# Decoder layer in full-precision parts: the last pair's steps in the down run, and pair 6's sums, moved to other rows

## The chip, the cores and the metric

One core of one Trainium2 chip runs the kernel. The metric is device time in microseconds of one execution, the median over several executions. A core has TensorE (PE: matmuls into the accumulators in PSUM; PEld is its weight load), VectorE (DVE), ScalarE (ACT), GpSimd (POOL), the queues of SyncE (SP) that issue DMAs, and 16 DMA engines. Each engine works through its own list of instructions in order; semaphores hold an instruction back until what it reads is there.

## The reference, cut to what matters

A decoder layer over 256 tokens of width 2048: a normalised input projection, attention over 8 heads beside a pooling mixer, an output projection, and a gated feed-forward part with a causal convolution of width 3 over the tokens. The change lies in that last part:

```python
def conv_ffn(h, w_up, conv_w, conv_b, w_down):
    u = h @ w_up                                   # (256, 2 * 5632)
    u_pad = jnp.pad(u, ((0, 0), (CONV_WIDTH - 1, 0), (0, 0)))
    y = conv_b
    for i in range(CONV_WIDTH):
        y = y + conv_w[i] * u_pad[:, i:i + S]
    gate, val = jnp.split(y, 2, axis=-1)
    return (jax.nn.silu(gate) * val) @ w_down      # (256, 2048)
```

## The kernel before

**Precision.** All matmuls run on numbers split in two: a high part (a copy rounded by ScalarE) and a low part (the number less its high part, by VectorE). A product is high x high, high x low and low x high. This holds for weights (`wh` at L184, `wl` at L190) and for activations (`hid[..., 0, :]` at L849, `hid[..., 1, :]` at L874).

**Thirds.** The 44 feature blocks of the feed-forward part are done in three thirds of 8, 8 and 6 pairs (a pair is 256 hidden features). A third has an **up run**, in which each pair has a block for its gate and a block for its value (four steps each, TensorE lines L271 and L273), and then a **down run** for the two halves `nb` of the output columns (TensorE line L904). The first step of a down run is called the border here.

**Seven products.** Where a pair is one of `sevens`, its two by two block of products is done with seven instead of eight, on sums of activation blocks and of weight blocks. The sums of the weights are made during the up run and go through memory (`mixed`); the sums of the activations are made by `left_sums`: four subtractions and additions on `y` (L889), a high part on ScalarE (L890) and a low part on VectorE (L891). In the first two thirds pairs 1 to 7 are such, in the order 1, 2, ..., 7, and pair 0 comes last with eight products; in the last third pairs 0 to 4 are such in one half and 0 to 3 in the other, and its last pair, 5, is not. A seven-product pair takes two steps in the down run, one with a weight tile of 2048 columns (`sum`: four products, 12 matmuls) and one of 1536 columns (`rest`: three products, 9 matmuls). An eight-product pair has one tile of 2048 columns.

**Weights.** One weight tile is a row of the plan. At the step at which row c starts on TensorE, the loop at the end of `layer` puts the high part of row c + 3 on ScalarE's list and then the low part of row c + 2 on VectorE's. When the low part is done, the buffer of the raw tile (five in all in this phase) is free, and SyncE issues the next load into it. There are 4 buffers for high and 3 for low parts. All weights come this way, so the order of the loads follows VectorE's order.

**The order is written by hand.** `later(n, f)` puts f at the step n after the one in hand; what is due at a step is put on the engines' lists behind the weights' parts of that step. (In an up run a row takes two steps, and only its first step counts: `later(2, ...)` is one row on. In a down run each seven-product row is one step.) `deferred` holds what is put on at the beginning of the next step, behind what is due there. `pending` holds ScalarE work that waits for the next time that an accumulator is emptied (`add_halves`, L540 and L543), and `firsts` what goes ahead of the weights' parts at a given step.

**A value block** (`value`) ends with `conv_in` (L540, L543, L801): the accumulator is emptied into `u`. Then come `conv` (six instructions on ScalarE, L812 and L814), `taps` (two additions on VectorE, L822), the product with the gate (L848), hid's high part (L849) and low part (L874), and, for a seven-product pair, `left_sums`. For the last pair of a third (`end`) all of it after `conv_in` falls into the down run. In `value`, `at_once` chooses between two orders; it is given by `g >= g1 - 2` inside a lambda. The steps after the border at which the last pair's parts are put on, as the code runs:

| part | thirds 1 and 2 | third 3 |
|---|---|---|
| conv | 0 | 2 and 4 (halves) |
| taps | 4 | 6 |
| gate product, hid's high part | 6 | 7 |
| hid's low part | 8 | 8 |
| four sums, their high part | 9 | - |
| low part of the sums | 11 | - |

The next to last seven-product pair of a third ahead of it (pair 6; pair 4 in the last third) has its four sums four steps before the border; their high part waits in `pending` for the next emptied accumulator, at the step before the border, and their low part comes at the border ahead of the weights (thirds 1 and 2, by `firsts`) or one step behind it (third 3).

Of the kernel before, what the change touches and what calls it, by code (L numbers as in the profile page):

```python
# [25 lines left out]
AF = mybir.ActivationFunctionType  # L26
# [3 lines left out]
P = 128  # L30
D = 2048
S = 256
# [5 lines left out]
NF = DFF // P  # L38
# [62 lines left out]
def layer(ctx: ExitStack, tc: tile.TileContext, xT, wts, mix, par, rel_d, ident_d, icnt_d, out):  # L101
    nc = tc.nc
# [15 lines left out]
    def small(name):  # L118
        return sm.tile([P, 512], F32, name=name, tag="small")
# [3 lines left out]
    def col(c):  # L123
        return pv[:, c:c + 1]
# [10 lines left out]
    late, free, place = {}, [f"raw{i}" for i in range(RAWS)], {}  # L135
# [185 lines left out]
    ps = small("ps_start")  # L321
# [277 lines left out]
    hold, splits, now, agenda, firsts, pending = set(), [], [0], {}, {}, []  # L599
    where = []  # L600

    def later(n, f):
        agenda.setdefault(now[0] + n, []).append(f)
# [25 lines left out]
    def after(u, f):  # L629

        hooks.append((u, f))
# [81 lines left out]
    def scratch(name):  # L713
        return late["pool"].tile([P, 2, S], F32, name=name, tag="fs", bufs=2)
# [82 lines left out]
    def conv_in(ps):  # L797

        s = scratch("fs")
        add_halves(s, ps)  # L800
        nc.vector.tensor_tensor(late["u"][:, :, 2:], s, late["rrow"][:, None, :].to_broadcast([P, 2, S]), op=OP.mult)  # L801

    def conv(f0_, which, apart=None):

        u = late["u"]
        y = late["pool"].tile([P, 2, S], F32, name="y", tag=f"y{which}")
        z = [scratch("z") for _ in range(2)]

        def half_of(m):
            f = f0_ + m  # L810
            cw = [col(C_CW + i * 2 * NF + f) for i in range(3)]
            nc.scalar.activation(y[:, m, :], u[:, m, 2:], AF.Identity, scale=cw[2], bias=col(C_CB + f))  # L812
            for i in range(2):
                nc.scalar.activation(z[i][:, m, :], u[:, m, 1 - i:1 - i + S], AF.Copy, scale=cw[1 - i])  # L814
        half_of(0)
        later(apart, lambda: half_of(1)) if apart else half_of(1)
        return y, z

    def taps(y, z):
# [18 lines left out]
            later(2, lambda: rest(parts))  # L838
        deferred.append(start)

    def value(ps, g, j, seven, end, at_once):
        conv_in(ps)

        def join(y):
            if j == 0:
                late["hid"] = keep.tile([P, KT, 2, S], F32R, name="hid", tag="c")
            hid, ks = late["hid"], slice(2 * j, 2 * j + 2)
            nc.vector.tensor_tensor(y, y, late["gate"], op=OP.mult)  # L848
            pending.append(lambda: nc.scalar.activation(hid[:, ks, 0, :], y, AF.Copy))  # L849
            if end:  # L850
                pending.pop()()
            later(1 if end and at_once else 2, lambda: rest2(y, hid, ks))

        def rest(parts):
            y = taps(*parts)
            if end:
                later(1 if at_once else 2, lambda: join(y))
            else:
                join(y)

        def start():
            if end and at_once:
                later(2, apart)
                return
            parts = conv(NF + 2 * g, 1)
            later(4 if end else 2, lambda: rest(parts))

        def apart():
            parts = conv(NF + 2 * g, 1, 2)
            later(4, lambda: rest(parts))  # L870
        deferred.append(start)

        def rest2(y, hid, ks):
            nc.vector.tensor_tensor(hid[:, ks, 1, :], y, hid[:, ks, 0, :].bitcast(F32), op=OP.subtract)  # L874
            if seven:
                f = lambda: late.__setitem__(("S", j), left_sums(y, end, at_once))
                later(1, f) if end else f()

    def left_sums(y, alone, at_once):

        s = y.rearrange("p a (b n) -> p (a b) n", n=P)
        if alone:
            pair = [late["pool"].tile([P, n], F32R, name="sums7", tag=tag)[:, :512] for n, tag in ((516, "u"), (512, "y0"))]
        else:
            parts = block("sums", F32R)
            pair = [parts[:, :512], parts[:, 512:]]
        pair = [t.rearrange("p (b n) -> p b n", n=P) for t in pair]
        for out_, a, b, op in ((3, 3, 1, OP.subtract), (1, 0, 1, OP.subtract), (0, 3, 0, OP.add), (2, 2, 0, OP.subtract)):
            nc.vector.tensor_tensor(s[:, out_, :], s[:, a, :], s[:, b, :], op=op)  # L889
        pending.append(lambda: nc.scalar.activation(pair[0], s, AF.Copy))  # L890
        low_part = lambda: nc.vector.tensor_tensor(pair[1], s, pair[0].bitcast(F32), op=OP.subtract)  # L891
        if alone:
            pending.pop()()
            later(2, low_part)
        elif at_once:
            later(5, low_part)
        else:
            firsts.setdefault(now[0] + 4, []).append(low_part)
        return pair

    def product(ps, left, right, first, last):
        (ah, al), (wh, wl) = left, right
# [85 lines left out]
    for n, ((g0, g1), sevens) in enumerate(zip(THIRDS, SEVEN)):  # L988
        ups = []
        for g in range(g0, g1):  # L990
            ups.append(feat_block(lambda: late["h"], XK, lambda ps, g=g: gate(ps, g)))
            ups.append(feat_block(lambda: late["h"], XK,
                                  lambda ps, g=g, j=g - g0, sevens=sevens, end=g == g1 - 1: value(ps, g, j, any(j in s for s in sevens), end, g >= g1 - 2)))
        u0 = len(steps)
        steps += [h for b in ups for h in b]
        if n == 0:
            for q in range(4):
                after(u0 + 2 + 3 * q, lambda q=q: x2_turn(q))
        for nb in range(2):
            run = {"n": nb * 1024, "end": n == 2 and nb == 1}  # L1000

            def done(t, lo, m, run=run, n=n, nb=nb):
                x2 = late["x2"][:, t, run["n"] + lo:run["n"] + lo + m]
                c = run["c"][t]
                if m == 1024:
                    parts = [(c[b], x2[:, b * 512:(b + 1) * 512]) for b in range(2)]
                else:
                    parts = [(c[lo // 512], x2)]
                for b, (ps, x) in enumerate(parts):
                    add = lambda ps=ps, x=x: nc.vector.tensor_tensor(x, ps, x, op=OP.add)  # L1010
                    later(3, add) if not nb and t and b else add()
                if n == 2:
                    k = min(m, 768 - lo) if nb and t else m
                    store = lambda: nc.sync.dma_start(out[:, t, run["n"] + lo:run["n"] + lo + k], x2[:, :k])
                    store() if nb else later(9, store)

            run["done"] = done
            run["x2"] = lambda t, b, run=run: late["x2"][:, t, run["n"] + b * 512:run["n"] + (b + 1) * 512]
            fresh0 = {(t, b) for t in range(NT) for b in range(2)}
            js = down_order(g1 - g0, sevens[nb])  # L1020
            for j in js:
                def chunk(u, j=j, nb=nb, run=run, sevens=sevens[nb], js=js, fresh0=fresh0, end=n == 2 and nb == 1):
                    if j == js[0]:
                        run["left"] = set(fresh0)
                        pair = [acc("ps_down") for _ in range(2)]
                        ones_ = [[f("ps_down") for f in (aux, small)] for _ in range(2)]
                        twos = [[t[:, b, :] for b in range(2)] for t in pair]
                        if nb:
                            (p6, p7), (p5, p1), (c10, c00), (c01, c11) = twos + ones_
                            run["c"] = [[c00, c01], [c10, c11]]  # L1030
                        else:
                            run["c"], ((p6, p7), (p5, p1)) = ones_, twos
                        run["p"] = p1, p5, p6, p7
                        run["spare"] = twos[0][0]
                    if j in sevens:
                        seven_mixed(u, j, run, j == sevens[0])
                    else:
                        eight_products(u, j, run, run["left"], j == js[-1], end and j == js[-1])
                        run["left"] = set()
                if j == js[-1]:  # L1040
                    hold.add(len(steps))
                steps.append([chunk])
                steps.append([lambda u, j=j, run=run, sevens=sevens[nb]: j in sevens and
                              seven_rest(u, j, run, j == sevens[0], j == sevens[-1])])
# [3 lines left out]
    n = len(steps)  # L1048
# [113 lines left out]
```

## Time and profile before

| | |
|---|---|
| median of 3 runs | 991.66 us (991.54 to 993.82) |
| the profiled execution | 990.43 us |
| its span, first to last instruction | 988.6 us |
| TensorE busy | 978.5 us, 99% |
| VectorE busy | 882.1 us, 89% |
| ScalarE busy | 630.1 us, 64% |
| granted TensorE clock | 1.00 |
| borders (first L904 matmul of a third) | 458.50, 713.77, 925.51 us |

Times in rows of the profile are microseconds from the start of the span. A row of the timeline has start, duration, engine, line, operation, the tiles written and read, shapes and count, and, where the engine sat idle before it, how long and what ended that. Instructions of one line in a row are merged into one row with their count. A matmul's duration there is longer than the distance to the next, since matmuls are pipelined: distances between starts are what counts. A row of the windows view has, for a stretch, its length, busy time and count of PE, PEld, DVE, ACT and POOL, the granted clock, the DMA engines' share and GB/s. A row of the waits view has who waited for whom, total, times and longest. A row of DMA issues has count, size and median time from issue to landing.

### The profile page before, as it was taken

The numbers are of one execution on the slowest core, as the hardware profiler recorded it, in microseconds if no ns is written. First come the engines' busy times: TensorE is split into PE (matmuls) and PEld (weight loads), VectorE is DVE, ScalarE is ACT, GpSimd is POOL, SyncE is SP. The second block draws the span as 40 slices with busy tenths as digits, with TensorE's granted clock in tenths as the row PEclk, the third lists the DMA queues.
The fourth block names the chain that finished last, engine by engine and source line by source line (L and its number), as shares of the span: only waits on it lengthen the run. The fifth ranks groups of instructions, "written<-read, shape, count | busy, mean of one in ns | idle before, by whom it ended". The sixth has DMA issues, their size and how long they took to land.

```text
span 988.6 us, 13621 instructions
## 1 busy us (share of the span) xinstructions
PE 978.5 (99%) x5249; PEld 844.6 (85%) x5249; DVE 882.1 (89%) x958; ACT 630.1 (64%) x736; POOL 61.3 (6%) x120
## 2 busy tenths in 40 slices
PE   9999999999999999999999999999999999999998
PEld 7888888898888888888788888888887888888887
DVE  6777859988888999998998999999899999999898
ACT  6555445544557766777666666776776746677762
POOL 0202322200002310000000000000000000000000
PEclk9999999999999999999999999999999999999999
DMA  9859878689878899976999999898689989998694
GB/s 355 311 205 344 293 243 287 207 326 390 303 266 304 312 392 394 370 296 251 363 335 362 349 389 367 336 355 333 260 314 323 398 332 347 369 388 329 219 350 163
DMA packets 52577, 317.08 MB, mean 321 GB/s; under 512 B 7112, under 2 KB 9800, under 8 KB 20256
## 3 DMA queue, kind: packets, MB, share of 16 engines
q1 hardware_dynamic: 47824, 304.28, 81.3%
q0 software_dynamic: 4688, 11.94, 4.2%
q8 instruction: 41, 0.67, 0.3%
q14 instruction: 24, 0.20, 0.1%
HBM read 269.13 MB, written 47.06 MB: 320 GB/s over the span
## 4 chain that ended last, share of the span: by engine, by line
PE 96%; DVE 2%; issue 1%; DMA 0%; ACT 0%; SPq 0%; DVEq 0%
PE ps_feat L271 41%; PE ps_feat L273 21%; PE ps_down L904 20%; PE ps_tok L259 9%; PE ps_val L249 4%; DVE wl L190 1%; PE ps_pool L280 1%; PE ps_s L492 1%; DMA raw<-in_wts 0%; ACT wh L184 0%; PE ps_av L528 0%; DVE y L889 0%; PE ps_av L530 0%; PE ps_val L240 0%; DVE x L1010 0%
## 5 line engine op out<-in xcount | busy, mean ns | idle before, releaser
L271 PE MATMUL ps_feat<-x2h,wh 128*128 128x512 f32 x1406 | 478.2, 389 | 0.0
L190 DVE TENSOR_TENSOR wl<-raw,wh 128x2048 fp32r<-128x2048 f32 (+1 forms) x182 | 394.0, 2176 | 12.9 <-ACT wh L184 7.5
L184 ACT ACTIVATE wh<-raw 128x2048 fp32r<-128x2048 f32 (+1 forms) x182 | 331.2, 1829 | 102.5 <-DMA raw<-in_wts 50.4
L273 PE MATMUL ps_feat<-x2h,wl 128*128 128x256 f32 x1408 | 388.6, 276 | 0.0
L271 PEld LDWEIGHTS ps_feat<-x2h,wh 128*128 128x128 f32 x1406 | 263.9, 188 | 54.4
L273 PEld LDWEIGHTS ps_feat<-x2h,wl 128*128 128x128 f32 x1408 | 264.3, 188 | 0.0
L904 PE MATMUL ps_down<-wh,hid 128*128 128x512 f32 (+1 forms) x338 | 116.1, 387 | 0.0
L162 DVE TENSOR_TENSOR wl<-raw,wh 128x2048 fp32r<-128x2048 f32 (+3 forms) x44 | 82.9, 1894 | 35.2 <-ACT wh L161 26.4
L904 PE MATMUL ps_down<-wh,sums 128*128 128x512 f32 x296 | 104.5, 390 | 3.5 <-DVE sums L891 3.5
L540 ACT ACTIVATE fs<-ps_feat 128x512 f32<-128x512 f32 x52 | 31.0, 597 | 105.6 <-DVE y L822 52.3
L271 PE MATMUL ps_feat<-cat,wh 128*128 128x512 f32 x256 | 87.3, 389 | 0.0
L814 ACT ACTIVATE z<-u,pv 128x256 f32<-128x256 f32 x176 | 79.3, 498 | 3.5 <-DVE x L947 3.5
L259 PE MATMUL ps_tok<-wh,xh 128*128 128x512 f32 x256 | 80.1, 391 | 0.0
L161 ACT ACTIVATE wh<-raw 128x2048 fp32r<-128x2048 f32 (+3 forms) x44 | 69.4, 1597 | 13.9 <-DMA raw<-in_wts 10.1
L904 PEld LDWEIGHTS ps_down<-wh,hid 128*128 128x128 f32 x338 | 63.3, 188 | 13.2
L273 PE MATMUL ps_feat<-cat,wl 128*128 128x256 f32 x256 | 70.7, 276 | 0.0
L904 PEld LDWEIGHTS ps_down<-wh,sums 128*128 128x128 f32 x296 | 55.4, 188 | 15.5 <-DVE sums L891 4.2
L904 PE MATMUL ps_down<-wl,hid 128*128 128x512 f32 (+1 forms) x169 | 65.4, 387 | 0.0
L822 DVE TENSOR_TENSOR y<-y,z 128x512 f32<-128x512 f32 x88 | 60.6, 688 | 4.4
L904 PE MATMUL ps_down<-wl,sums 128*128 128x512 f32 x148 | 58.7, 397 | 1.2 <-DVE wl L190 1.2
L259 PEld LDWEIGHTS ps_tok<-wh,xh 128*128 128x128 f32 x256 | 48.1, 188 | 10.0
L271 PEld LDWEIGHTS ps_feat<-cat,wh 128*128 128x128 f32 x256 | 48.1, 188 | 10.0
(184 smaller groups left out, 1061.8 us busy)
## 6 DMA issues: line engine op xcount, KB each, us to landing
raw<-in_wts SPq DMA_DIRECT2D x141, 1024.0 KB, 7.7
raw<-in_mix SPq DMA_DIRECT2D x37, 1024.0 KB, 7.4
mixed<-raw SPq DMA_DIRECT2D x37, 1024.0 KB, 7.4
raw<-mixed SPq DMA_DIRECT2D x37, 1024.0 KB, 6.9
raw<-in_wts SPq DMA_DIRECT2D x37, 768.0 KB, 6.3
raw<-in_wts SPq DMA_DIRECT2D x4, 512.0 KB, 6.5
x2d<-x2x POOLq DMA_DIRECT2D x4, 512.0 KB, 8.0
x<-x2d POOLq DMA_DIRECT2D x32, 64.0 KB, 6.8
```

Source lines behind the costliest of these rows:

```text
L161: nc.scalar.activation(wh, w, AF.Copy)
L162: nc.vector.tensor_tensor(wl, w, wh.bitcast(F32), op=OP.subtract)
L184: nc.scalar.activation(w, raws[c][:, :width(c)], AF.Copy)
L190: nc.vector.tensor_tensor(wl, raws[c][:, :width(c)], wh.bitcast(F32), op=OP.subtract)
L249: nc.tensor.matmul(ps[b][:, t, :], xh[:, k, a, ts], w[:, ws], start=False, stop=(k == KT - 1 and n == 2), skip_group_check=True)
L259: nc.tensor.matmul(ps[:, t, :], act[:, k0 + k, a, ts], w[:, ws], start=(first and k == 0 and n == 0), stop=(last and k == 1 and n == 2))
L271: nc.tensor.matmul(ps, wh[:, ws], act[:, k, :, :], start=(bool(first) and n == 0), stop=False, skip_group_check=True)
L273: nc.tensor.matmul(ps[:, S:], wl[:, ws], act[:, k, 0, :], start=False, stop=(last and n == len(ks) - 1), skip_group_check=True)
L540: nc.scalar.activation(dst, ps[:, :, S:], AF.Copy)
L814: nc.scalar.activation(z[i][:, m, :], u[:, m, 1 - i:1 - i + S], AF.Copy, scale=cw[1 - i])
L822: nc.vector.tensor_tensor(y, y, t, op=OP.add)
L904: nc.tensor.matmul(ps, a, w, start=(first and n == 0), stop=(last and n == 2), skip_group_check=True)
```

## The change

The last pair of each third gets one order, and its ScalarE parts are put on one step behind the VectorE work that they read:

| part | before, thirds 1 and 2 | before, third 3 | after, all thirds |
|---|---|---|---|
| conv | 0 | 2 and 4 | 0 |
| taps | 4 | 6 | 3 |
| gate product | 6 | 7 | 4 |
| hid's high part (ScalarE) | 6 | 7 | 5 |
| hid's low part | 8 | 8 | 6 |
| four sums | 9 | - | 7 |
| their high part (ScalarE) | 9 | - | 8 |
| their low part | 11 | - | 9 |

The pair before the last (`left == 1`, now bound when the lambda is made: pair 6, in the last third pair 4) has both parts of its sums put on two steps before the border. Pairs before it stay as they were.

```diff
-    def conv(f0_, which, apart=None):
+    def conv(f0_, which):
...
-    def value(ps, g, j, seven, end, at_once):
+    def value(ps, g, j, seven, end, late_sums):
...
-            pending.append(lambda: nc.scalar.activation(hid[:, ks, 0, :], y, AF.Copy))
-            if end:
-                pending.pop()()
-            later(1 if end and at_once else 2, lambda: rest2(y, hid, ks))
+            high_part = lambda: nc.scalar.activation(hid[:, ks, 0, :], y, AF.Copy)
+            later(1, high_part) if end else pending.append(high_part)
+            later(2, lambda: rest2(y, hid, ks))
 
         def rest(parts):
             y = taps(*parts)
-            if end:
-                later(1 if at_once else 2, lambda: join(y))
-            else:
-                join(y)
+            later(1, lambda: join(y)) if end else join(y)
 
         def start():
-            if end and at_once:
-                later(2, apart)
-                return
             parts = conv(NF + 2 * g, 1)
-            later(4 if end else 2, lambda: rest(parts))
-
-        def apart():
-            parts = conv(NF + 2 * g, 1, 2)
-            later(4, lambda: rest(parts))
+            later(3 if end else 2, lambda: rest(parts))
         deferred.append(start)
 
         def rest2(y, hid, ks):
             nc.vector.tensor_tensor(hid[:, ks, 1, :], y, hid[:, ks, 0, :].bitcast(F32), op=OP.subtract)
-            if seven:
-                f = lambda: late.__setitem__(("S", j), left_sums(y, end, at_once))
-                later(1, f) if end else f()
-
-    def left_sums(y, alone, at_once):
+            if seven and end:
+                later(1, lambda: left_sums(y, j, 1, 2))
+            elif seven:
+                left_sums(y, j, *((2, 2) if late_sums else (None, None)))
+
+    def left_sums(y, j, n_high, n_low):
...
-        pending.append(lambda: nc.scalar.activation(pair[0], s, AF.Copy))
+        high_part = lambda: nc.scalar.activation(pair[0], s, AF.Copy)
         low_part = lambda: nc.vector.tensor_tensor(pair[1], s, pair[0].bitcast(F32), op=OP.subtract)
-        if alone:
-            pending.pop()()
-            later(2, low_part)
-        elif at_once:
-            later(5, low_part)
+        if n_high:
+            later(n_high, high_part)
+            later(n_low, low_part)
         else:
+            pending.append(high_part)
             firsts.setdefault(now[0] + 4, []).append(low_part)
...
-                                  lambda ps, g=g, j=g - g0, sevens=sevens, end=g == g1 - 1: value(ps, g, j, any(j in s for s in sevens), end, g >= g1 - 2)))
+                                  lambda ps, g=g, j=g - g0, sevens=sevens, left=g1 - 1 - g: value(ps, g, j, any(j in s for s in sevens), left == 0, left == 1)))
```

More of the change, by code (lines that the diff above doesn't have):

```diff
@@ L807, in conv @@
         z = [scratch("z") for _ in range(2)]
-        def half_of(m):
+        for m in range(2):
             f = f0_ + m
@@ L814, in half_of @@
                 nc.scalar.activation(z[i][:, m, :], u[:, m, 1 - i:1 - i + S], AF.Copy, scale=cw[1 - i])
-        half_of(0)
-        later(apart, lambda: half_of(1)) if apart else half_of(1)
         return y, z
@@ L874, in rest2 @@
             nc.vector.tensor_tensor(hid[:, ks, 1, :], y, hid[:, ks, 0, :].bitcast(F32), op=OP.subtract)
-            if seven:
-                f = lambda: late.__setitem__(("S", j), left_sums(y, end, at_once))
-                later(1, f) if end else f()
-    def left_sums(y, alone, at_once):
+            if seven and end:
[3 more added lines that the diff above has]
+    def left_sums(y, j, n_high, n_low):
         s = y.rearrange("p a (b n) -> p (a b) n", n=P)
-        if alone:
+        if j == 7:
             pair = [late["pool"].tile([P, n], F32R, name="sums7", tag=tag)[:, :512] for n, tag in ((516, "u"), (512, "y0"))]
@@ L886, in left_sums @@
             pair = [parts[:, :512], parts[:, 512:]]
-        pair = [t.rearrange("p (b n) -> p b n", n=P) for t in pair]
+        late["S", j] = pair = [t.rearrange("p (b n) -> p b n", n=P) for t in pair]
         for out_, a, b, op in ((3, 3, 1, OP.subtract), (1, 0, 1, OP.subtract), (0, 3, 0, OP.add), (2, 2, 0, OP.subtract)):
             nc.vector.tensor_tensor(s[:, out_, :], s[:, a, :], s[:, b, :], op=op)
-        pending.append(lambda: nc.scalar.activation(pair[0], s, AF.Copy))
+        high_part = lambda: nc.scalar.activation(pair[0], s, AF.Copy)
         low_part = lambda: nc.vector.tensor_tensor(pair[1], s, pair[0].bitcast(F32), op=OP.subtract)
-        if alone:
-            pending.pop()()
-            later(2, low_part)
-        elif at_once:
-            later(5, low_part)
+        if n_high:
+            later(n_high, high_part)
+            later(n_low, low_part)
         else:
+            pending.append(high_part)
             firsts.setdefault(now[0] + 4, []).append(low_part)
-        return pair
     def product(ps, left, right, first, last):
```

## The prediction

> **What bounds the kernel now.** I read the page first, then TensorE's waits, then the three engines in order of time around the borders where an up run ends and a down run begins.
>
> ```profile
> span 988.6 us, 13621 instructions
> PE 978.5 (99%) x5249; PEld 844.6 (85%) x5249; DVE 882.1 (89%) x958; ACT 630.1 (64%) x736; POOL 61.3 (6%) x120
> ...
> PE ps_down L904 <- DVE sums L891: 3.5, 2, 1.8
> PE ps_down L904 <- DVE wl L190: 1.2, 2, 0.6
> ```
>
> TensorE is busy 99% of the span; idle time to win stands at two places, the down runs of the first two thirds, where the products of pair 7 wait for the low part of their sums (L891) and for weights (L190). "Row k" is the k-th weight tile of a down run, from 0: pair p has rows 2p-2 (sums) and 2p-1 (rest). The wl row below is the second matmul of a sums row, the first to need VectorE's low part of the weights.
>
> ```profile
> 458.50 0.40 PE L904 MATMUL ps_down<-wh,sums 128*128 128x512 f32 x1
> 458.73 0.40 PE L904 MATMUL ps_down<-wl,sums 128*128 128x512 f32 x1
> ...
> 473.42 0.39 PE L904 MATMUL ps_down<-wl,sums 128*128 128x512 f32 x1
> ...
> 478.18 0.39 PE L904 MATMUL ps_down<-wl,sums 128*128 128x512 f32 x1
> ...
> 490.88 0.74 PE L904 MATMUL ps_down<-wh,sums 128*128 128x512 f32 x2 [1.77 <-DVE sums L891]
> ```
> ```profile
> 714.01 0.40 PE L904 MATMUL ps_down<-wl,sums 128*128 128x512 f32 x1
> ...
> 746.15 0.72 PE L904 MATMUL ps_down<-wh,sums 128*128 128x512 f32 x2 [1.77 <-DVE sums L891]
> ```
>
> Pairs 4 and 5 run unstalled: 478.18 - 473.42 = 4.76 us a pair, 0.23 from one matmul to the next. Without stalls pair 7's third matmul would start at 458.73 + 6 x 4.76 + 0.23 = 487.52; it starts at 490.88: **3.36 us lost** at the first border. At the second, 714.01 + 28.79 = 742.80 against 746.15: 3.35. All that can be won is 6.7 us.
>
> VectorE (L190 the low half of weights, L822 taps, L848 gate product, L874 hid, L889/L891 sums):
>
> ```profile
> 459.33 0.69 DVE L543 TENSOR_TENSOR fs<-ps_feat,fs 128x512 f32<-128x512 f32 x1 [2.29 <-ACT fs L540]
> ...
> 460.66 0.69 DVE L891 TENSOR_TENSOR sums<-y,sums 128x512 fp32r<-128x512 f32 x1
> 461.26 3.95 DVE L190 TENSOR_TENSOR wl<-raw,wh 128x2048 fp32r<-128x2048 f32 x2
> 466.13 6.16 DVE L190 TENSOR_TENSOR wl<-raw,wh 128x2048 fp32r<-128x2048 f32 x3 [0.92 <-ACT wh L184]
> 472.21 1.41 DVE L822 TENSOR_TENSOR y<-y,z 128x512 f32<-128x512 f32 x2
> 473.54 3.96 DVE L190 TENSOR_TENSOR wl<-raw,wh 128x1536 fp32r<-128x1536 f32 x2
> 477.42 0.68 DVE L848 TENSOR_TENSOR y<-y 128x512 f32<-128x512 f32 x1
> 478.02 1.75 DVE L190 TENSOR_TENSOR wl<-raw,wh 128x1536 fp32r<-128x1536 f32 x1
> 480.60 2.29 DVE L190 TENSOR_TENSOR wl<-raw,wh 128x2048 fp32r<-128x2048 f32 x1 [0.83 <-ACT wh L184]
> 482.81 0.68 DVE L874 TENSOR_TENSOR hid<-y,hid 128x512 fp32r<-128x512 f32 x1
> ...
> 485.08 1.26 DVE L889 TENSOR_TENSOR y<-y 128x128 f32<-128x128 f32 x4
> 486.27 3.96 DVE L190 TENSOR_TENSOR wl<-raw,wh 128x2048 fp32r<-128x2048 f32 x2
> 490.14 0.69 DVE L891 TENSOR_TENSOR sums<-y,sums 128x512 fp32r<-128x512 f32 x1
> ```
>
> From 459.33 on VectorE is idle for 0.92 and 0.83 us alone: here it, not TensorE, sets the pace. Both idles end on ScalarE:
>
> ```profile
> 458.70 0.60 ACT L540 ACTIVATE fs<-ps_feat 128x512 f32<-128x512 f32 x1 [3.63 <-PE ps_feat L273]
> 459.19 0.62 ACT L890 ACTIVATE sums<-y 128x512 fp32r<-128x512 f32 x1
> ...
> 461.62 0.58 ACT L812 ACTIVATE y<-u,pv 128x256 f32<-128x256 f32 x1
> ...
> 464.20 6.45 ACT L184 ACTIVATE wh<-raw 128x2048 fp32r<-128x2048 f32 x4
> ...
> 478.13 0.63 ACT L849 ACTIVATE hid<-y 128x512 fp32r<-128x512 f32 x1 [1.60 <-DVE y L848]
> 478.67 5.08 ACT L184 ACTIVATE wh<-raw 128x2048 fp32r<-128x2048 f32 x3
> ```
>
> The first: row 4's high half (464.20) stands behind the convolution (461.62 to 464.20). The second: row 10's (478.67) stands behind the hid copy, which waited 1.60 us for the product of L848. The convolution is whole, right at the border: `g >= g1 - 2` in the lambda is evaluated when it runs, with the last third's g1 = 22, so in the first two thirds the branches of at_once are never taken, for pair 6 neither.
>
> **The change, part by part.** No instruction is added or removed; all are moved, so the sum is one of order.
>
> *Pair 6's sums.* Both parts go to two steps before the border. ScalarE's copy (0.52 to the next start) leaves 459.19 and fills the 3.63 us that it is idle before 458.70; VectorE's low part (460.66 to 461.26, 0.60) leaves the border and fills 2.29 us of idle time. Cost there nothing; without that cover 0.6. It stands behind the high half of row 2 on ScalarE, and gate 7's taps stand behind it.
>
> *Pair 7 on ScalarE.* The convolution stays where it is in two thirds. The hid copy and the sums' copy go one step behind VectorE, so row 10's high half no longer waits for the product: the 0.83 goes. In exchange the sums' copy stands behind row 11's high half, and so behind that tile's landing (below).
>
> *Pair 7 on VectorE*: taps from step 4 to 3, product 6 to 4, hid's low part 8 to 6, the four sums 9 to 7, their low part 11 to 9. Prices, start to start: a 2048-wide weight row 2.21 and a 1536-wide 1.66 (6.08 for three, 3.87 for two), taps 1.33, product 0.60, hid the like, 0.61, four sums 1.19, low part 0.60. New order at the first border:
>
> - rows 2 and 3 at 460.66 (461.26 now), done 464.53. Row 4's high half starts at 464.20 - 0.52 = 463.68, ends 1.92 later, 465.60; so row 4 at 465.63.
> - row 5, taps, then row 6 at 465.63 + 2.21 + 1.66 + 1.33 = 470.83, done at 473.12. TensorE wants it at 458.73 + 3 x 4.76 = 473.01: with 0.05 from end to start, **0.15 late**.
> - product, rows 7 and 8, hid, row 9, four sums: 473.04 + 0.60 + 1.66 + 2.21 + 0.61 + 1.66 + 1.19 = 480.97 for row 10, done 483.26; wanted at 482.53: **0.78 late in all**.
> - row 11, low part at 484.84, row 12 at 485.44, done 487.73; wanted at 487.29 + 0.78 = 488.07: in time, and the sums since 485.5.
>
> So the wait moves from the sums to row 10's weights and shrinks from 3.36 to 0.78: 2.58 won at the first border, 2.57 at the second, whose rows are the same. Loads are issued when a row's low half is done: rows 7 to 10 are asked for 0.5 sooner, row 11 0.8 later (it follows row 6), rows 12 and 13 0.1 later.
>
> ```profile
> raw<-mixed SPq DMA_DIRECT2D x37, 1024.0 KB, 6.9
> ```
>
> The tightest is row 8, asked for at 464.6 when row 3 is done: landed at 471.5, its high half done at 473.4 and the hid copy behind it at 474.0, against 475.30 for row 8's low half and 477.51 for hid's low part, which wait for them on VectorE with all later weights behind.
>
> *Last third.* Its last pair is no seven-product pair, but moves too; here at_once did hold, so the convolution, in halves at steps 2 and 4, moves whole to the border.
>
> ```profile
> 925.74 0.40 PE L904 MATMUL ps_down<-wl,sums 128*128 128x512 f32 x1
> ...
> 927.68 3.95 DVE L190 TENSOR_TENSOR wl<-raw,wh 128x2048 fp32r<-128x2048 f32 x2
> ```
>
> VectorE starts row 2 1.94 after TensorE's first wl, as it will at the first border (460.66 - 458.73 = 1.93); the order up to row 6 is the same, so the same **0.15 is lost**, where nothing is lost now. No sums follow; row 10 comes 1.19 sooner than there, in time.
>
> Sum: 2.58 + 2.57 - 0.15 = 5.0 us. The profiled execution took 990.43 (span 988.6, 1.8 around it); the median of the three runs, 991.66, lies 1.2 above it. I take the gain off the median: **986.6**.
>
> **Rivals.**
>
> *The later rows don't follow (987.8).* TensorE arrives 2.6 us sooner at rows past 13, and their weights hang on transfers.
>
> ```profile
> 477.60:482.40 4.80, 4.80 (x23) 3.98 (x22) 3.96 (x3) 4.27 (x4) 0.00 (x0) 1.00 1.03 424
> 515.00:540.00 25.00, 25.00 (x113) 20.67 (x112) 22.16 (x18) 16.71 (x11) 0.10 (x1) 1.00 0.97 388
> ```
> ```profile
> 530.22 2.29 DVE L190 TENSOR_TENSOR wl<-raw,wh 128x2048 fp32r<-128x2048 f32 x1 [1.09 <-ACT wh L184]
> ...
> 534.44 0.39 PE L904 MATMUL ps_down<-wl,hid 128*128 128x512 f32 x1
> ```
> ```profile
> 756.71 3.95 DVE L190 TENSOR_TENSOR wl<-raw,wh 128x2048 fp32r<-128x2048 f32 x2
> ...
> 761.05 0.39 PE L904 MATMUL ps_down<-wl,sums 128*128 128x512 f32 x1
> ```
>
> The DMA share (next to last) is 1.03 and 0.97. If no later row came sooner, the smallest leads would cap the gain: 534.44 - 532.51 = 1.93 in the first run, 761.05 - 759.00 = 2.05 in the second; 1.93 + 2.05 - 0.15 = 3.8. Against it: row 12 is done 0.8 sooner, and the loads behind it are asked for sooner by that. [...]
>
> *VectorE still waits for ScalarE (989.3).* If row 4 isn't sooner (0.5) and the 0.83 comes back elsewhere, row 10 ends 1.33 later, 2.11 late: 1.25 and 1.24 won, minus 0.15, 2.3. Against it: the hid copy then follows a product done four steps ahead of row 10.
>
> *No wait is left (985.0)*: 6.7 won. It needs VectorE 0.8 us faster over 23 us; its two idles end on ScalarE, which has slack, but the convolution is not moved.
>
> *Slower (over 991.7).* Place: step 8, ScalarE: sums' copy behind row 11's high half, behind its landing. VectorE's low part, rows 12 and 13 and the loads that these release stand behind it. Row 11 is asked for at 473.2.
>
> ```profile
> raw<-in_wts SPq DMA_DIRECT2D x37, 768.0 KB, 6.3
> ```
>
> Landed at 479.5, high half 1.4, copy 0.6: 481.5 against 484.84, 3.3 spare. Each microsecond past that costs one. It turns the gain into a loss from 3.3 + 2.6 on, a landing 12 us after its issue at both borders: twice the median.
>
> **How the numbers follow.** Forecast 0.46, later rows 0.20, ScalarE 0.19, no wait 0.08, slower 0.07. 0.3% (about what a measurement here tells from no change) is 3.0 us, so faster means below 988.7: 0.46 + 0.20 + 0.08 = 0.74; same 0.19; slower 0.07. The range runs from the full gain, 984.9, to the ScalarE case, 989.5; the forecast's own is 986.0 to 987.4.
>
> **What would show it.** Right: no wait on L891 at pair 7; a wait on wl L190 at pair 6's sums row of 0.4 to 0.8 in two thirds, and at pair 4's of 0.1 to 0.2 in all three; no 0.83 idle before row 10 on VectorE; L891 and L890 once each before the border instead of behind it. Wrong: TensorE waiting past row 13 (later rows), VectorE idle on L184 or L890 between rows 4 and 12 (ScalarE, slower), or the time moving without these rows.

## The result and the profile after

The changed kernel takes **986.72 us** (median of 19 runs, 985.08 to 994.43) where the kernel before, timed beside it, takes 993.59 (19 runs, 991.31 to 997.42): a ratio of **0.9932, 95% interval 0.9919 to 0.9946**. The forecast was 986.6, faster. The profiled execution after has a span of 985.8 us, against 988.6 before: the two profiles differ by 2.8 us, the medians by 6.9. Why the medians lie further apart than the profiles was the question for the experiments.

TensorE's waits in the changed kernel (who waited for whom: total, times, longest):

```profile
PE ps_val L240 <- ACT wh L161: 1.4, 2, 0.9
PE ps_start L323 <- DVE ones L311: 1.1, 1, 1.1
PE ps_down L889 <- DVE wl L190: 0.9, 3, 0.3
PE ps_feat L268 <- DVE sd L942: 0.3, 1, 0.3
```

The wait for the sums (3.5 us, now line L878) is gone. TensorE at the first border, in order of time: the first matmul that needs a low half of the weights, that of pair 4 (row 6), that of pair 6 (row 10), and pair 7's third matmul as the first of two.

```profile
459.66 0.40 PE L889 MATMUL ps_down<-wl,sums 128*128 128x512 f32 x1
...
474.14 0.50 PE L889 MATMUL ps_down<-wl,sums 128*128 128x512 f32 x1
...
484.26 0.50 PE L889 MATMUL ps_down<-wl,sums 128*128 128x512 f32 x1 [0.31 <-DVE wl L190]
...
489.41 0.62 PE L889 MATMUL ps_down<-wh,sums 128*128 128x512 f32 x2
```

With 4.76 us a pair, row 6 is due at 459.66 + 14.28 = 473.94 and comes 0.20 late; row 10 is due at 483.46 and comes 0.80 late; pair 7's third matmul is due at 488.45 and comes 0.96 late, where it was 3.36 late before. VectorE at the same border (L819 taps, L845 product, L860 hid's low part, L876 four sums, L878 low part of sums):

```profile
456.55 0.69 DVE L878 TENSOR_TENSOR sums<-y,sums 128x512 fp32r<-128x512 f32 x1
...
460.31 0.69 DVE L543 TENSOR_TENSOR fs<-ps_feat,fs 128x512 f32<-128x512 f32 x1 [1.74 <-ACT fs L540]
...
461.64 3.96 DVE L190 TENSOR_TENSOR wl<-raw,wh 128x2048 fp32r<-128x2048 f32 x2
466.59 3.96 DVE L190 TENSOR_TENSOR wl<-raw,wh 128x2048 fp32r<-128x2048 f32 x2 [1.00 <-ACT wh L184]
470.47 1.41 DVE L819 TENSOR_TENSOR y<-y,z 128x512 f32<-128x512 f32 x2
471.80 2.28 DVE L190 TENSOR_TENSOR wl<-raw,wh 128x2048 fp32r<-128x2048 f32 x1
474.00 0.68 DVE L845 TENSOR_TENSOR y<-y 128x512 f32<-128x512 f32 x1
474.61 3.95 DVE L190 TENSOR_TENSOR wl<-raw,wh 128x1536 fp32r<-128x1536 f32 x2
478.48 0.68 DVE L860 TENSOR_TENSOR hid<-y,hid 128x512 fp32r<-128x512 f32 x1
...
480.75 1.26 DVE L876 TENSOR_TENSOR y<-y 128x128 f32<-128x128 f32 x4
481.92 3.95 DVE L190 TENSOR_TENSOR wl<-raw,wh 128x2048 fp32r<-128x2048 f32 x2
485.80 0.68 DVE L878 TENSOR_TENSOR sums<-y,sums 128x512 fp32r<-128x512 f32 x1
```

Pair 6's low part stands at 456.55, ahead of the border, and the idle time behind it has shrunk from 2.29 to 1.74. The 0.83 us before row 10 is gone; one idle is left, 1.00 before row 4, which still waits for ScalarE behind the convolution. From 466.59 to 492.5, behind the last step that was moved, VectorE works without a gap. ScalarE:

```profile
455.90 0.62 ACT L877 ACTIVATE sums<-y 128x512 fp32r<-128x512 f32 x1
...
464.65 6.46 ACT L184 ACTIVATE wh<-raw 128x2048 fp32r<-128x2048 f32 x4
...
474.72 0.63 ACT L846 ACTIVATE hid<-y 128x512 fp32r<-128x512 f32 x1 [0.63 <-DVE y L845]
...
477.42 1.93 ACT L184 ACTIVATE wh<-raw 128x2048 fp32r<-128x2048 f32 x1 [0.68 <-DMA raw<-mixed]
480.41 1.49 ACT L184 ACTIVATE wh<-raw 128x1536 fp32r<-128x1536 f32 x1 [1.07 <-DMA raw<-in_wts]
482.04 0.64 ACT L877 ACTIVATE sums<-y 128x512 fp32r<-128x512 f32 x1
```

The hid copy (474.72) still waits 0.63 us for the product, which the forecast did not have; it is done 3.1 us before hid's low part (478.48), and costs nothing. Row 10's high half (477.42) now waits for its landing, not for pair 7's product, and is done 2.6 us before VectorE takes it. The sums' copy stands behind row 11's high half (480.41), which waits 1.07 us for its landing: done at 482.7, 3.1 us ahead of the low part at 485.80.

Stretches of all profiles, from TensorE's starts: the first border, the three down runs (the third to the end of the span), and how many of the first two down runs have a stretch at half clock in them.

| kernel | first border | down 1 | down 2 | third to end | half clock |
|---|---|---|---|---|---|
| before | 458.50 | 81.16 | 81.13 | 63.13 | 0 |
| before, again | 458.73 | 82.75 | 82.49 | 62.80 | 2 |
| before, wait filled | 458.18 | 81.14 | 81.51 | 62.83 | 0 |
| pair 6 alone | 459.48 | 80.67 | 82.07 | 63.41 | 1 |
| last pair alone | 460.14 | 79.14 | 79.10 | 63.71 | 0 |
| changed | 459.43 | 78.65 | 79.24 | 63.71 | 0 |
| changed, again | 459.11 | 79.08 | 78.62 | 63.13 | 0 |
| changed, third time | 458.61 | 78.63 | 78.67 | 64.52 | 0 |
| changed, copies at once | 459.58 | 79.68 | 79.65 | 63.85 | 0 |
| changed, no four sums | 458.65 | 78.02 | 78.02 | 63.19 | 0 |
| changed, all one later | 459.26 | 78.08 | 78.08 | 62.84 | 0 |
| the same, again | 458.37 | 78.13 | 78.26 | 62.85 | 0 |

The second up run takes 174.12 us in all of them; the third 130.6 to 130.7 in all but one, where the matmuls start some 4% further apart at a granted clock of 1.00 (135.76, copies at once). Why stays open; that profile's span is not used below.

### The profile page after: what moved, and what is told of

Read it like the earlier page. It is cut to its first block, busy times and chain, and to the rows that moved or that the text cites. A ratio compares the mean times of both kernels' runs of the same rounds, so it can differ in the third digit from the quotient of the medians.

```text
span 985.8 us, 13614 instructions
## 1 busy us (share of the span) xinstructions
PE 978.6 (99%) x5249; PEld 844.7 (86%) x5249; DVE 881.2 (89%) x958; ACT 631.7 (64%) x736; POOL 61.6 (6%) x120
## 4 chain that ended last, share of the span: by engine, by line
PE 96%; DVE 2%; DMA 1%; ACT 0%; issue 0%; SPq 0%; DVEq 0%; ACTq 0%
PE ps_feat L271 41%; PE ps_feat L273 21%; PE ps_down L889 19%; PE ps_tok L259 9%; PE ps_val L249 4%; DMA raw<-in_wts 1%; DVE wl L190 1%; PE ps_pool L280 1%; PE ps_s L492 1%; PE ps_av L528 0%; ACT wh L184 0%; PE ps_av L530 0%; DVE y L876 0%; PE ps_val L240 0%; DVE x L995 0%
## 5 line engine op out<-in xcount | busy, mean ns | idle before, releaser
L819 DVE TENSOR_TENSOR y<-y,z 128x512 f32<-128x512 f32 x88 | 60.6, 688 | 4.2
```

What stands on the lines that cost most here:

```text
L819: nc.vector.tensor_tensor(y, y, t, op=OP.add)
```

## The experiments

**Both kernels once more.** No edit.

> The kernel before, unchanged, taken once more. My theory puts the gain into the two stalls at pair 7 (3.4 us each in the profile of before): the same two stalls, 3.3 to 3.5 us, and a ratio of 1.000 within 0.002. The rival (the gain comes from parts that differ from run to run, since the medians moved by 6.9 us and the two profiled spans by 2.8): the stretch from the start to the first border, 458.5 us in the first profile, differs here by 1 us or more, and so may the stalls.

> The changed kernel, unchanged, taken once more. My theory: ratio 0.992 to 0.996; no wait on L878 at pair 7; row 6 about 0.2 late and row 10 0.7 to 0.9 late in all in two thirds, and first to second border 252.8 us, second to third 209.9 as in its first profile. The rival that parts outside the borders moved: the stretch to the first border differs from 459.4 by 1 us or more.

Measured: before 992.9 us (11 runs), ratio 0.9998 (0.9986 to 1.001). The waits for the sums are the same (3.5 in total, 1.8 the longest), and the stretch to the first border differs by 0.2 us: the rival's place is wrong. But the span is 991.5, 2.9 us longer, and the windows view shows where (length; PE, PEld, DVE, ACT, POOL; granted clock; DMA share; GB/s):

```profile
487.80:491.50 3.70, 1.35 (x6) 0.57 (x5) 3.70 (x4) 3.70 (x3) 0.00 (x0) 1.00 0.93 368
491.50:494.90 3.40, 3.40 (x10) 2.64 (x9) 1.76 (x1) 0.72 (x1) 0.00 (x0) 0.50 0.93 355
```

Right behind the stall the granted clock is 0.50 for 3.40 us, and 10 matmuls stand in them. In order of time:

```profile
491.11 0.90 PE L904 MATMUL ps_down<-wh,sums 128*128 128x512 f32 x2 [1.77 <-DVE sums L891]
491.81 0.63 PE L904 MATMUL ps_down<-wl,sums 128*128 128x512 f32 x1
492.24 0.63 PE L904 MATMUL ps_down<-wh,sums 128*128 128x512 f32 x1
```

Starts are 0.43 us apart instead of 0.23. The first down run takes 82.75 instead of 81.16, the second 82.49 instead of 81.13: 1.4 to 1.6 us for a stretch at half clock, which the profile that the prediction read happened not to have. The changed kernel again: 986.03 us, ratio 0.9927 (0.9915 to 0.994), no half clock, no wait for the sums; first to second border 253.2 where 252.8 was expected, second to third 209.2 for 209.9.

**The wait filled.** TensorE is kept at work while it waits, and nothing else moves (the tile of zeros is made once, at 206 us, by one more instruction of VectorE):

```diff
-        product(p6, s2, t2, first, False)
+        if j == 7 and not run["n"]:
+            (ah, al), (wh, wl) = s2, t2
+            zero = late["zero"]
+            nc.tensor.matmul(p6, ah, wh, start=first, stop=False, skip_group_check=True)
+            for _ in range(3):
+                nc.tensor.matmul(p6, zero, wh, start=False, stop=False, skip_group_check=True)
+            nc.tensor.matmul(p6, ah, wl, start=False, stop=False, skip_group_check=True)
+            for _ in range(8):
+                nc.tensor.matmul(p6, zero, wh, start=False, stop=False, skip_group_check=True)
+            nc.tensor.matmul(p6, al, wh, start=False, stop=False, skip_group_check=True)
+        else:
+            product(p6, s2, t2, first, False)
```

> The kernel before, with 3 and 8 more matmuls by a tile of zeros (their products add nothing to the sum) in front of pair 7's second and third matmul in the first half of the down run of two thirds, so that TensorE works through most of its 0.8 and 2.0 us of waiting; no engine's order is touched. The profiles of before differ by the granted clock: 0.5 for 3.41 us behind the stall at no border, at both, at one. Theory that the stall itself sets off the half clock, and that this is the part of the gain beyond the 5.0 us: no row at half clock before the end, first to second border 255.3 us as in the undisturbed profile, and 1.5 to 2.5 us less than before in the median (ratio 0.9975 to 0.9985). Rival, the clock falls whatever TensorE does there, or the medians differ for another reason: ratio 1.000 and half clock in some stretch again.

Measured: 990.79 us against 992.64 beside it, ratio **0.9986 (0.9973 to 0.9998)**, and no half clock in its profile. Two windows of the first profile of before, where the clock held too, and then of this kernel:

```profile
487.50:491.00 3.50, 1.13 (x5) 0.39 (x4) 3.50 (x4) 3.50 (x3) 0.00 (x0) 1.00 0.84 322
491.00:494.50 3.50, 3.50 (x16) 2.85 (x17) 3.21 (x2) 2.10 (x2) 0.00 (x0) 1.00 0.94 328
```
```profile
487.50:491.00 3.50, 3.50 (x16) 2.43 (x15) 3.50 (x4) 2.94 (x3) 0.00 (x0) 1.00 0.96 355
491.00:494.50 3.50, 3.50 (x17) 2.87 (x16) 3.21 (x2) 2.69 (x2) 0.00 (x0) 1.00 0.88 326
```

The down runs are those of the first profile of before (81.14 and 81.51): the wait is as long, only TensorE isn't idle in it. Of the six borders with the idle wait (before twice, pair 6 alone), three have a stretch at half clock behind them (granted clock of the whole profile 0.997 and 0.998); of the 18 borders without it (this kernel and eight profiles of changed kernels, where the waits views show no wait for VectorE's weights at a border over 0.6 us), none (1.000 in all nine profiles). So the idle wait sets off the half clock in some executions; 1.85 us by the medians, 1.4 by the ratio, with an interval of 0.2 to 2.7, hang on it.

What decides in which executions the clock falls is not shown. The length of the stall does not tell them apart: the waits are 0.6 and 1.8 us long in both profiles of before, and around the stall TensorE is idle for 2.37 us of 487.50 to 491.00 in the first, where the clock held, and for 2.35 us of 487.80 to 491.50 in the second, where it fell.

The clock of the runs says how often it happens. By estimate one such stretch takes 0.0017 off the mean granted clock of a run (half of 3.40 in 990 us). Of 73 runs of the kernel before whose clock is on record, 8 have 0.999 or 1.000, with a median of 991.13 us; 36 have 0.998, about one stretch, and 29 less; the median of all is 992.87, 1.7 us more. All 34 runs of the changed kernel have 0.999 or 1.000. The profile that the prediction read was one of the few without. Filling the wait does not keep the clock up in every run: two of the 12 runs of this kernel have 0.998 (993.14 and 994.98 us), and so have three of the ten with the copies at once (below). No profile of those five runs was kept, so where their clock fell stays open.

**Pair 6's sums alone.** Built on the kernel before:

```diff
+        elif late_sums:
+            later(2, high_part)
+            later(2, low_part)
```

> Only the sums of pair 6 (pair 4 in the last third) two steps ahead of the border, the last pair in the order of before. My theory: VectorE and ScalarE start the down run 0.6 and 0.5 us sooner, and everything up to pair 7's low part follows: its wait shrinks by 0.5 to 0.6 us at two borders, nothing in the last third: ratio 0.999, first to second border 254.7. The rival that pair 6's sums are most of the gain: 2 us or more a border. The rival that they give nothing: 255.3 and no shift of row 4's low half.

Measured: 992.49 us, ratio 1.000 (0.999 to 1.001), which can't tell 1 us, and half clock at one border. The profile can: the first down run, without half clock, is 80.67 against 81.16, 0.49 less. The expectation had the place wrong: pair 7's wait did not shrink,

```profile
PE ps_down L906 <- DVE sums L891: 3.5, 2, 1.8
```

because TensorE's small stalls at rows 2, 4 and 10 went, so that it came to pair 7 sooner by as much as the sums did.

**The last pair alone.** Built on the changed kernel:

```diff
-                left_sums(y, j, *((2, 2) if late_sums else (None, None)))
+                left_sums(y, j, None, None)
```

> Only the last pair's new order; pair 6's sums as in the first two thirds of before (high part at the step before the border, low part at it), in the last third too. My theory: the same order on VectorE 0.5 to 0.6 us later: row 4 about 0.2 late, row 6 0.7 late, row 10 1.3 late in all at two borders, no wait for the sums; 2.1 us won a border, 0.6 lost in the last third: ratio 0.9965, first to second border 253.2. The rival that VectorE isn't the bound up to row 10: row 10 as late as in the changed kernel (0.8), and the same time as that.

Measured: 988.17 us, ratio 0.9948 (0.9935 to 0.996). Down runs 79.14 and 79.10, 2.0 less than before each, and the third stretch 0.6 to 0.9 longer, where 0.6 was expected. Row 10:

```profile
460.38 0.40 PE L889 MATMUL ps_down<-wl,sums 128*128 128x512 f32 x1
...
485.46 0.50 PE L889 MATMUL ps_down<-wl,sums 128*128 128x512 f32 x1 [0.31 <-DVE wl L190]
```

485.46 - (460.38 + 23.80) = 1.28 late, expected 1.3: what VectorE does at the border later, TensorE pays at row 10. The ratio is lower than the expected 0.9965, for here too the half clock is gone: all five runs have a granted clock of 1.000.

**ScalarE's copies at VectorE's own step.** Built on the changed kernel:

```diff
-            later(1, high_part) if end else pending.append(high_part)
+            high_part() if end else pending.append(high_part)
...
-                later(1, lambda: left_sums(y, j, 1, 2))
+                later(1, lambda: left_sums(y, j, 0, 2))
```

(with `left_sums` putting the copy on at once for 0).

> The changed kernel, but the last pair's two ScalarE copies are put on at VectorE's own step (4 and 7) and not one behind (5 and 8). Theory: the hid copy then stands before row 8's high half and waits for the product; row 8's high half starts 0.9 to 1.2 us after the landing and VectorE idles for about 0.9 before row 8; row 10 is 1.7 us late in all instead of 0.8, 0.9 lost at each of two borders (first to second border 253.7 to 254.1 us), ratio 0.9945. Rival, that the step behind gives nothing, since ScalarE is only 64% busy: as the changed kernel, 252.8 to 253.2 and 0.993.

ScalarE and VectorE of this kernel, first border:

```profile
474.93 0.63 ACT L846 ACTIVATE hid<-y 128x512 fp32r<-128x512 f32 x1 [3.66 <-DVE y L845]
475.47 5.07 ACT L184 ACTIVATE wh<-raw 128x2048 fp32r<-128x2048 f32 x3
```
```profile
477.40 2.29 DVE L190 TENSOR_TENSOR wl<-raw,wh 128x2048 fp32r<-128x2048 f32 x1 [0.90 <-ACT wh L184]
```

The hid copy waits 3.66 us for the product with row 8's high half behind it, and VectorE idles 0.90 before row 8 (477.40), as expected. The down runs take 79.68 and 79.65, 0.9 more than the changed kernel's mean of 78.8; first to second border 253.80. The rival (nothing lost, since ScalarE has idle time) falls: the step behind is worth 0.9 us a border. The runs spread from 987.81 to 994.44, and the ratio's interval (0.9947 to 0.9988) settles nothing.

**Without pair 7's four sums.** Built on the changed kernel:

```diff
-            nc.vector.tensor_tensor(s[:, out_, :], s[:, a, :], s[:, b, :], op=op)
+            if j != 7:
+                nc.vector.tensor_tensor(s[:, out_, :], s[:, a, :], s[:, b, :], op=op)
```

> The changed kernel without the four additions of pair 7's sums (1.19 us of VectorE at two borders): the parts are taken from the unsummed product, so the seven products of that pair are of other numbers. Theory that VectorE's work up to row 10 is what is left of the stall: row 10 in time, row 6 as late as in the changed kernel (0.2 to 0.3), 0.6 less a border: first to second 252.2 us. Rival, row 10 waits for its landing or ScalarE: as late as before, 252.8 to 253.2.

Measured: 985.1 us, ratio 0.9929 (0.991 to 0.9948), down runs 78.02, first to second border 252.14. Row 10 here:

```profile
458.88 0.40 PE L890 MATMUL ps_down<-wl,sums 128*128 128x512 f32 x1
...
483.02 0.39 PE L890 MATMUL ps_down<-wl,sums 128*128 128x512 f32 x1
```

483.02 - 482.68 = 0.34, all of it from row 6. With 1.19 us of VectorE taken away ahead of row 10, row 10's own wait is gone: VectorE's work is what is left of the stall.

**All of the last pair one step later.** Built on the changed kernel, and timed twice, the second time with the changed kernel on the same chip:

```diff
-            later(3 if end else 2, lambda: rest(parts))
+            later(4 if end else 2, lambda: rest(parts))
```

> The changed kernel with all of the last pair's steps from the taps on one later (taps 4, product 5, hid's copy 6, hid's low part 7, four sums 8, copy 9, low part 10). The arithmetic of the prediction: before row 6 no taps (row 6 in time, in all thirds), before row 10 taps, product and hid but no four sums (done 482.0 against 482.5, in time), row 12 at 487.1 in time, low part of the sums 487.7 against 487.5: 0.25 late there, in place of 0.8 to 0.95. So 0.5 to 0.7 less a border and 0.3 in the last third: first to second 252.2, second to third 209.2, ratio 0.0012 below the changed kernel's. Rival: the rows past 13, which lead by only 0.05 to 0.5 us in the changed kernel, take it back: rows 16 to 19 wait, and the time is the changed kernel's.

> All of the last pair's steps one later, beside the changed kernel on one chip. Theory (VectorE's work ahead of row 10 sets what is left of the stall): row 6 and row 10 in time, 0.4 late at pair 7 alone, first to second border 252.2 and second to third 208.7 us again, 1.2 to 2.2 us less than the changed kernel in the median. Rival (the difference between the two calls was the chip's): the two medians within 0.6 us.

> The changed kernel beside the next one on one chip. Expected: 986 to 986.7 us, row 10 0.8 to 1.0 late in all at two borders, no stretch at half clock before the end.

Measured: 984.17 us, ratio 0.9913 (0.9899 to 0.9926), and again 984.32, ratio 0.9931 (0.9905 to 0.9956), beside the changed kernel's 986.47, ratio 0.9938 (0.9919 to 0.9958). The intervals of the ratios overlap; the medians are 2.15 us apart on this chip, within the 1.2 to 2.2 expected, and 1.86 between the runs before, which were on two chips. VectorE and TensorE:

```profile
466.43 6.16 DVE L190 TENSOR_TENSOR wl<-raw,wh 128x2048 fp32r<-128x2048 f32 x3 [1.00 <-ACT wh L184]
472.51 1.41 DVE L819 TENSOR_TENSOR y<-y,z 128x512 f32<-128x512 f32 x2
...
480.58 2.28 DVE L190 TENSOR_TENSOR wl<-raw,wh 128x2048 fp32r<-128x2048 f32 x1
482.78 1.26 DVE L876 TENSOR_TENSOR y<-y 128x128 f32<-128x128 f32 x4
```
```profile
459.49 0.40 PE L889 MATMUL ps_down<-wl,sums 128*128 128x512 f32 x1
...
488.57 0.72 PE L889 MATMUL ps_down<-wh,sums 128*128 128x512 f32 x2
```

The taps stand behind row 6 and the four sums behind row 10; pair 7's third matmul is 488.57 - 488.28 = 0.29 late, expected 0.25. The down runs are 78.1 to 78.3, and the third stretch is 62.84 and 62.85, what the kernel before needs and 0.3 to 1.7 less than the changed kernel. Against the changed kernel's means that is 0.7 us less in each of the first two down runs and 0.9 in the third stretch, 2.3 in all, in agreement with the medians. The rival (later rows take it back) falls: this is the best version here.

## Why the prediction was right, and where it was not

**Right: the order on VectorE.** Measured from the first matmul with a low half (458.73 in the prediction, 459.66 here), row 4 was to start at +6.90, row 6 at +12.10, row 10 at +22.24, the low part at +26.11 and row 12 at +26.71. They start at +6.93, +12.14, +22.26, +26.14 and +26.74 (486.40). Row 6 was to be 0.15 late and is 0.20; row 10 0.78, and is 0.80. The rows that would show it came: no wait for the sums, no 0.83 us idle, the new waits at pairs 4 and 6, row 12 in time.

**A little small: what a stall costs.** Pair 7's third matmul is 0.96 late, not 0.78: the matmul that ends a stall takes 0.50 instead of 0.40, and the next starts later by about 0.1, which the sum did not have. So the first two down runs gained 81.16 - 78.79 = 2.37 and 81.13 - 78.84 = 2.29 (means of three profiles) against 2.58 and 2.57. Single profiles lose a little elsewhere too: one at row 4 (0.13 late), one at row 17 and at the end of its second down run (0.17 and 0.41).

**Wrong in size: the last third.** The sum lost 0.15 there. The third stretch is 63.13 and 62.80 us in the two profiles of before and 63.71, 63.13 and 64.52 in those of the changed kernel: 0.8 us lost in the mean. Row 6 is 0.18 late in all three profiles, as forecast, 0.29 with the slower matmul behind it. The step that failed is the one that closes the sum there: "No sums follow; row 10 comes 1.19 sooner than there, in time", with nothing put down for the rows behind. VectorE at this border, rows 4 to 7 before, then rows 6 and 7 in the profile with 64.52:

```profile
932.15 7.82 DVE L190 TENSOR_TENSOR wl<-raw,wh 128x2048 fp32r<-128x2048 f32 x4
```
```profile
931.67 1.41 DVE L819 TENSOR_TENSOR y<-y,z 128x512 f32<-128x512 f32 x2
933.00 2.28 DVE L190 TENSOR_TENSOR wl<-raw,wh 128x2048 fp32r<-128x2048 f32 x1
935.20 0.68 DVE L845 TENSOR_TENSOR y<-y 128x512 f32<-128x512 f32 x1
935.81 3.95 DVE L190 TENSOR_TENSOR wl<-raw,wh 128x1536 fp32r<-128x1536 f32 x2
```

Before, rows 4 to 7 followed one another here; now the taps stand ahead of row 6 and the product ahead of row 7. The loads that these two release, of rows 11 and 12, go out 14.68 and 16.95 us after the border instead of 12.82 and 14.49. TensorE then waits at row 13 in two of the three profiles (0.42 and 0.62 us by the starts of its matmuls), and in one of them at row 12 too (0.44). In the profile with 64.52, ScalarE first, then VectorE, then TensorE:

```profile
946.16 1.49 ACT L184 ACTIVATE wh<-raw 128x1536 fp32r<-128x1536 f32 x1 [1.47 <-DMA raw<-in_wts]
947.56 0.58 ACT L922 ACTIVATE sa<-ps_down 128x512 f32<-128x512 f32 x1
```
```profile
948.17 0.69 DVE L938 TENSOR_TENSOR sb<-sa,ps_down 128x512 f32<-128x512 f32 x1 [1.15 <-ACT sa L922]
...
951.82 1.75 DVE L190 TENSOR_TENSOR wl<-raw,wh 128x1536 fp32r<-128x1536 f32 x1
```
```profile
953.62 0.50 PE L889 MATMUL ps_down<-wl,hid 128*128 128x512 f32 x1 [0.28 <-DVE wl L190]
```

Row 12's high half waits for its landing, the copy that empties an accumulator (L922) stands behind it, VectorE idles 1.15 us for that copy, and row 12's low half, behind what follows the copy, comes late. It is the mechanism of the slower rival, a copy behind a high half behind its landing, at another place: not at step 8 in two thirds, where 3.1 us were spare, but where the last third's first half ends. Row 12's load is issued 16.95 us after the border in each of the three profiles, and lands at 23.79, 24.66 and 25.42: in this order the third stretches are 63.13, 63.71 and 64.52. Before, it was issued at 14.49 and landed at 22.02 and 22.44. So the moved order uses up the spare time, and the length of one transfer then decides how much is lost. With all steps one later it is issued at 16.36 and lands at 22.89 and 23.32, and the loss is gone (62.84).

**Missed: the half clock. The number was luck.** The prediction took 5.0 us off 991.66, the median of three runs. Both are too small, and by nearly the same: the 19 runs timed with the result have a median of 993.59, 1.93 more, and the medians are 6.87 us apart, 1.87 more than 5.0. So 986.6 was hit with two errors that lie against each other. By the stretches the moved work is worth 2.37 + 2.29 - 0.82 = 3.8 us, not 5.0. What brought the medians 6.1 to 6.9 us apart is, beyond that, mostly the half clock behind the stall: 1.4 to 1.6 us at a border where it falls, 1.4 to 1.85 us in the whole by the filled wait. 3.8 + 1.85 = 5.7; the rest lies within what the stretch to the first border (458.2 to 460.1) and the intervals leave open. The trace that the prediction read had none of it (one profiled execution in which the clock held at both borders), and its own time, 990.43, lay under the lowest of the 19 runs; that it stood 1.2 under the median was noted as a plain difference, though it was the hint. "All that can be won is 6.7 us" counted idle time alone and falls too: the best version here is 8.3 to 8.5 us under the kernel before.

**The rivals.** Later rows: no stall past row 13 in the first down run; in the second only the one at row 17. In the last third this rival did find a place, at rows 12 and 13. VectorE waiting for ScalarE: idle only before row 4, 1.00 us, as the forecast had it; the experiment with the copies at once shows what it would have cost. All but 0.2 to 0.4 us of the wait at a border goes with VectorE's order of the last experiments.

## What to carry to other kernels

Where an engine that isn't the bound feeds the bound in a fixed order, write down for each piece of its work when it is due, and fit the movable work in behind the pieces that are due first: moving it as early as possible only moves the wait to the next piece, and one step later was better here. Give a copy that waits for another engine a place behind the work that doesn't, also where its own engine is mostly idle. Where an order is moved, follow the loads that it releases to the end of the run, not only to the last moved piece. A stall of the bound engine can cost more than its length (here 1.4 to 1.6 us more, at three of six borders): look at the granted clock of several executions before taking one profile as the base.

## What the runs showed of the hardware

A stall of TensorE of 0.8 and 2.0 us with one matmul between was followed in three of six cases by a stretch at half the granted clock (0.50 from 491.50 to 494.90 us, 3.40 us, in the second profile of before), in which matmuls of 128x512 start 0.43 us apart instead of 0.23; such a stretch cost 1.4 to 1.6 us. What sets it off in one execution and not in another was not shown. Matmuls by zeros in the wait kept the clock at 1.00 in the profile, and at 0.999 or 1.000 in ten of 12 runs.

In the changed kernel the matmul behind a stall of TensorE lasts 0.50 us instead of 0.40, and the next starts 0.34 us after it instead of 0.23 (474.14 to 474.48 and 484.26 to 484.60).
